# One of four weight sums of each gate/up set: from accumulating transfers to four GpSimd additions

## The chip, the core and the metric

The kernel runs on one core of a Trainium2 chip. The metric is the device time of one execution in microseconds (us), the median of several executions; lower is better. The engines are named as in the profile: PE is TensorE's matmul, PEld its weight loads, DVE is VectorE, ACT is ScalarE, POOL is GpSimd, SP is SyncE, which here only issues transfers.

## The reference

Two decoder layers over 256 tokens of width 1024 in float32. A layer adds to `h`, one after the other: half a SwiGLU feed-forward block (FFN1), a token mixer (differential attention in layer 0, a Mamba-2 scan in layer 1), a cross-attention into 256 memory tokens, and half a second SwiGLU block (FFN2). A last RMSNorm follows. There are thus four feed-forward blocks, and the change lies in them:

```
def rmsnorm(x, w):
    xf = x.astype(jnp.float32)
    y = xf * lax.rsqrt(jnp.mean(xf * xf, axis=-1, keepdims=True) + EPS)
    return (y * w.astype(jnp.float32)).astype(x.dtype)

def swiglu(h, w_gate, w_up, w_down):
    return (jax.nn.silu(h @ w_gate) * (h @ w_up)) @ w_down

    h = h + 0.5 * swiglu(rmsnorm(h, ffn1_norm[i]), ffn1_w_gate[i], ffn1_w_up[i], ffn1_w_down[i])
```

`w_gate` and `w_up` are 1024 x 2816, `w_down` is 2816 x 1024; all weights are read from DRAM once per execution, in float32.

## The kernel before

**Splitting.** A float32 product is made of three matmuls in a reduced format (L262 to L264): each operand is the sum of a `hi` and a `lo` part, and `hi*hi`, `hi*lo` and `lo*hi` are accumulated. A weight tile in SBUF, 128 x 2048 (`w`, L161, four blocks of 128 rows by 512 columns), is cut into *granules* of 128 x 1024. For each, ACT rounds the granule to `whi` (L224) and DVE subtracts it from the weights, `wlo = w - whi` (L225). PE then uses both. Four `whi` and four `wlo` buffers exist, so ACT and DVE can run some three granules ahead of PE, no more.

**Sets.** Gate and up projection are not multiplied one by one. For a group of 512 columns of each, `seven` makes a two by two block product with seven block products instead of eight: the columns of `w_up` are B11 (upper half of the rows) and B21 (lower half), those of `w_gate` are B12 and B22. Four sums of weights are needed:

- x1 = B11 + B12, by DVE into a new tile (L203, 128 x 2048, as soon as both are loaded);
- x2 = x1 + B22, by DVE in place (L203);
- x4 = x2 + B21, in x2's tile, by two transfers from DRAM that add to what lies in SBUF (L199, issued by POOL);
- x3 = B12 + B22, in B12's tile, by two such transfers as well (L199).

B22 is also loaded by itself (SP), since it is a factor of its own and the second operand of x2. The products come in the order B11, x1, x2, B22, x3, B21, x4, two granules each. Between these fourteen granules PE works on granules of other matrices ("hosts", `share` and `weave`): gate, up and down projection in ordinary form. There are 15 sets: three in the first FFN (column groups 2, 3, 4) and four in each other one (groups 1 to 4).

**What sets the order.** Each engine executes its own list in order. The lists come from the program order and a planner with due times (`pipe.after`), and are fixed when the kernel is built. Transfers into SBUF are issued by SP in its own order, each as soon as one of nine `w` buffers is free. POOL's list is short: the accumulating transfers, a power function on tiny tiles for the norms (L466, `rcol`), and additions in the attention (L930) and the scan (L1436 to L1440). DVE's list in a set holds, beside L203 and L225, operations that read a matmul result in PSUM: L831 and L837 (sums of products), L843 and L808 (gating), L859 (the `lo` part of the hidden activations).

Of the kernel before, what the change touches and what calls it, by code (L numbers as in the profile page):

```python
# [12 lines left out]
ALU = mybir.AluOpType  # L13
# [44 lines left out]
def trunk(ctx, tc, a, out):  # L58
    nc = tc.nc
# [15 lines left out]
    def acc(name):  # L75
        return pacc.tile([P, 512], F32, name=name, tag="acc")
# [4 lines left out]
    def work(name, n=512, dt=F32):  # L81

        return wk.tile([P, n], dt, name=name, tag="v", bufs=6) if n <= 256 else wk.tile([P, n], dt, name=name, tag="w")
# [24 lines left out]
    class Pipe:  # L108
# [4 lines left out]
        def after(self, us, f):  # L113
            self.q.append((self.t + us, f))
# [30 lines left out]
    class W:  # L145
# [6 lines left out]
        def load(self, k=None, nk=None):  # L152
            if k is None:
                if self.t is not None:
                    return
                k, nk = 0, self.nk
            if self.t is None:
                t = wp.tile([P, 2048], F32, name="w", tag="w")
                self.t = t[:, :self.nk * self.n].rearrange("p (k c) -> p k c", c=self.n)
            r0 = (self.k0 + k) * P  # L160
            nc.sync.dma_start(self.t[:, k:k + nk, :], self.src[r0:r0 + nk * P, self.c0:self.c0 + self.n]  # L161
                              .rearrange("(k p) c -> p k c", p=P))
# [17 lines left out]
    class Sum:  # L180
# [5 lines left out]
        def load(self):  # L186
            if self.t is not None:
                return
            self.l.load()
            if self.into is None:  # L190
                self.r.load()
                self.t = wp.tile([P, 2048], F32, name="w", tag="w").rearrange("p (k c) -> p k c", c=512)
            else:
                self.t = self.l.t
            w = self.r
            if self.into == "dma":
                for k in (0, 2):
                    r0 = (w.k0 + k) * P
                    nc.gpsimd.dma_start(self.t[:, k:k + 2, :], w.src[r0:r0 + 2 * P, w.c0:w.c0 + w.n]  # L199
                                        .rearrange("(k p) c -> p k c", p=P), accum_op=ALU.add)  # L200
            else:
                w.load()
                nc.vector.tensor_tensor(self.t, self.l.t, w.t, op=ALU.add)  # L203

    class Gran:

# [54 lines left out]
    def mm3(o, lh, ll, rh, rl, start, stop, onto=False):  # L261
        nc.tensor.matmul(o, lhsT=lh, rhs=rh, start=start, stop=False, skip_group_check=onto)  # L262
        nc.tensor.matmul(o, lhsT=lh, rhs=rl, start=False, stop=False, skip_group_check=onto)  # L263
        nc.tensor.matmul(o, lhsT=ll, rhs=rh, start=False, stop=stop, skip_group_check=onto)  # L264
# [93 lines left out]

    ONTO = {2: 0, 4: 0, 3: 1, 5: 1, 6: 1}

    def seven(b1, b2, x, mix, after, order=(0, 1, 2, 3, 5, 4, 6), second="dma"):

        b11, b21 = (W(b1[0], k, 4, b1[1], 512) for k in (0, 4))
        b12, b22 = (W(b2[0], k, 4, b2[1], 512) for k in (0, 4))
        x1 = Sum(b11, b12)
        x2 = Sum(x1, b22, second)
        x4 = Sum(x2, b21, "dma")
        x3 = Sum(b12, b22, "dma")
        banks = {}

        def a(t, h):
            return lambda k: tuple(v[:, t * P:(t + 1) * P] for v in pipe.need(x, 4 * h + k))

        def s(i):
            return lambda k: tuple(v[:, k * P:(k + 1) * P] for v in pipe.need(mix, i))
        plan = [(x1, s(0)), (b11, a(0, 0)), (b22, s(1)), (x2, s(2)), (b21, a(0, 1)), (x3, s(3)), (x4, a(1, 1))]
        out = []
        for i in order:
            w, lhs = plan[i]
            for k0 in (0, 2):  # L380
                def step(g, i=i, lhs=lhs, k0=k0):
                    if not k0:
                        banks[i] = banks[ONTO[i]] if i in ONTO else acc("seven")
                    for k in range(k0, k0 + 2):
                        lh, ll = lhs(k)
                        mm3(banks[i], lh, ll, g.hi[:, k - k0, :], g.lo[:, k - k0, :], k == 0 and i < 2, k == 3, onto=i in ONTO)
                        pipe.pe(0.68)
                    if k0:
                        for w in {0: (x2, x3), 3: (x4,)}.get(i, ()):
                            w.load()  # L390
                        after(i, banks)
                out.append((Gran(w.k0 + k0, 2, (w, 0, 512)), step))
        return out

    def share(hosts, s, counts):
        out, hosts = [], list(hosts)
        for i, n in enumerate(counts):
            out += hosts[:n] + s[2 * i:2 * i + 2]
            hosts = hosts[n:]
        return out + hosts  # L400
# [381 lines left out]
    def ffn_hidden(nm, l, norm, fin, tail, extra=None):  # L782
# [31 lines left out]
        def extras(c):  # L814
            for i in (2 * c, 2 * c + 1):
                if extra and i in extra:
                    extra[i]()

        def seven_fin(c):
            us, t = {}, {}  # L820

            def after(i, b):
                v = nc.vector

                def copy():
                    t[i] = work(f"p{i}")
                    nc.scalar.copy(t[i], b[i])

                def c12():
                    us[0] = t[3]  # L830
                    v.tensor_tensor(us[0], b[2], t[3], op=ALU.subtract)  # L831
                    nc.scalar.copy(b[2], t[1])
                    nc.scalar.activation(us[0], us[0], AF.Silu, scale=norm.col[:, 0:1])

                def c22():
                    us[1] = t[0]
                    v.tensor_tensor(t[0], t[0], b[5], op=ALU.subtract)  # L837
                    nc.scalar.activation(t[0], t[0], AF.Silu, scale=norm.col[:, 1:2])
                    if c == 4:
                        extras(6)  # L840

                def up(r):
                    v.scalar_tensor_tensor(us[r], b[i], norm.col[:, r:r + 1], us[r], op0=ALU.mult, op1=ALU.mult)  # L843
                    if r:
                        pipe.after(T["hid"], lambda: turn(c, [us[0], us[1]], 512))
                        extras(c)
                pipe.after(0.7, {0: copy, 1: copy, 3: copy, 2: c12, 5: c22, 4: lambda: up(0), 6: lambda: up(1)}[i])
            return after

        def turn(c, us, n):  # L850
            for i in range(0, n // P, 2):
                tp = v2(small_ps("htp"))
                for j in range(2):
                    for t in range(2):
                        nc.tensor.transpose(tp[:, j, t * P:(t + 1) * P], us[t][:, (i + j) * P:(i + j + 1) * P], ident)  # L855
                hi = v2(slot("hid_hi", F32R))
                lo = v2(slot("hid_lo", F32R))
                nc.scalar.copy(hi, tp)
                nc.vector.tensor_tensor(lo, tp, hi.bitcast(F32), op=ALU.subtract)  # L859
                for j in range(2):  # L860
                    hid[4 * c + i + j] = (hi[:, j, :], lo[:, j, :])
        wg, wu = a[nm + "_w_gate"][l], a[nm + "_w_up"][l]
        wide([(wg, 0, 512)], norm, "gate", gate_fin(0), **({} if units else dict(single=True, eng=nc.gpsimd)))
        c = HID // 512
# [19 lines left out]
            n += d0[i:j] + d1[i:j]  # L884
        steps = []
        for c, k in counts.items():
            s = seven((wu, c * 512), (wg, c * 512), norm.x, norm.s, seven_fin(c), (1, 0, 3, 2, 5, 4, 6), "dve")
            steps += share(n[:sum(k)], s, k)
            n = n[sum(k):]
        assert not n  # L890
# [3 lines left out]
    def ffn(nm, l, norm, nxt, extra=None):  # L894
        fin = upd(0.5, nxt)
        ffn_hidden(nm, l, norm, fin, lambda hid, wd: down(wd, 1, [(12, 4), (16, 4)], hid, [], 12, fin), extra)
# [218 lines left out]
    def cross_attention(l, norm, kv, nxt):  # L1115
# [86 lines left out]
        wkv = a["xa_w_kv"][l]  # L1202
        q = [g for c in (2, 0) for g in columns(a["xa_w_q"][l], c * 256, norm, "xq", [q_fin(c), q_fin(c + 1)])]
        weave(share(q, seven((wkv, 1024), (wkv, 1536), kv.x, kv.s, mv_fin()), [2, 1, 1, 2, 1, 1, 0]))
        out_b(a["xa_w_o"][l], KT, ot, upd(1.0, nxt), (4, 0))

# [329 lines left out]
    def last(norm):  # L1536
# [71 lines left out]
        def tail(hid_, wd):  # L1608
            hid.append(hid_)
            gr.extend(Gran(k, 2, (w, 0, 512)) for w in [W(wd, k, 4, 512, 512) for k in (12, 16)] for k in (w.k0, w.k0 + 2))  # L1610
            return [(gr[0], run)]
        ffn_hidden("ffn2", 1, norm, first_half, tail, {12: final_gain})
        units.append((gr[1:], run))

# [72 lines left out]
```

## Time and profile before

| | |
|---|---|
| median of 3 executions | 1257.75 us (1257.62 to 1258.05) |
| the profiled execution | 1258.38 us, of which the span is 1256.6 us |
| PE busy | 1247.1 us (99%), PEld 1071.7 us (85%) |
| DVE busy | 1057.2 us (84%) |
| ACT busy | 873.5 us (70%) |
| POOL busy | 162.5 us (13%) |
| transfers | 275.03 MB, of which 38.28 MB on the queue q0, which POOL feeds |
| granted TensorE clock | 0.999 |

A page of the profile gives busy time by engine, the span in 40 slices, the transfer queues, the chain of waits that ended last, groups of instructions by source line, and the transfers by issuer with their median time to landing. Other views show one engine's instructions in order of time, the waits added up by who waited for whom, and busy time within chosen windows. In a row of the timeline the first number is the start in us from the span's start, the second the duration, and what stands in brackets is the idle time of the engine before it and what ended that. Instructions that follow one another directly and have the same line and tiles are merged into one row, with their count.

### The profile page before, as it was taken

How to read it: one execution, taken by the hardware profiler on the slowest of the kernel's cores; microseconds unless marked ns; L12 is line 12 of the kernel's file. 1: busy time of each engine (PE TensorE's matmuls, PEld its weight loads, DVE VectorE, ACT ScalarE, POOL GpSimd, SP SyncE). 2: the span in 40 equal slices, each digit the busy share in tenths (PEclk: the TensorE clock that was granted, in tenths of full speed). 3: DMA queues.
4: the chain of work that ended last, by engine and by line, in shares of the span. 5: the costliest groups of instructions: out<-in, count | busy, mean ns of one | idle time of the engine just before them, and what ended most of it. 6: DMA issues, size and time to landing. Idle time of an engine off the chain costs nothing.

```text
span 1256.6 us, 18186 instructions
## 1 busy us (share of the span) xinstructions
PE 1247.1 (99%) x6751; PEld 1071.7 (85%) x6751; DVE 1057.2 (84%) x1451; ACT 873.5 (70%) x1388; POOL 162.5 (13%) x139
## 2 busy tenths in 40 slices
PE   9999999999999999999999999999999999999997
PEld 7888888788998888888888889999998898888886
DVE  6998787887787999887998976798898887898886
ACT  6676764686676776767776756777876775877772
POOL 1101102101101111110111000022233100011100
PEclk9999999999999999999999999999999999999999
DMA  9989976445776688987879977665636586489961
GB/s 330 301 255 259 314 256 208 137 165 170 222 214 170 165 252 260 293 246 234 240 198 268 311 247 221 192 193 168 201 134 185 169 246 182 157 251 256 258 190 34
DMA packets 161195, 275.03 MB, mean 219 GB/s; under 512 B 7209, under 2 KB 43730, under 8 KB 161106
## 3 DMA queue, kind: packets, MB, share of 16 engines
q1 hardware_dynamic: 137744, 229.75, 53.4%
q0 software_dynamic: 19744, 38.28, 17.7%
q10 hardware_dynamic: 3618, 5.84, 1.4%
q8 instruction: 53, 0.87, 0.3%
q14 instruction: 36, 0.29, 0.1%
HBM read 271.72 MB, written 2.13 MB: 218 GB/s over the span
## 4 chain that ended last, share of the span: by engine, by line
PE 94%; DMA 2%; DVE 2%; ACT 2%; issue 1%; POOLq 0%; POOL 0%; SPq 0%; ACTq 0%; DVEq 0%
PE out L262 9%; PE out L264 9%; PE out L263 9%; PE seven L263 8%; PE seven L262 8%; PE seven L264 8%; PE htp L855 1%; PE up L263 1%; PE up L264 1%; PE up L262 1%; PE xs L264 1%; PE xs L262 1%; PE xq L263 1%; PE xq L264 1%; PE xs L263 1%; PE xq L262 1%
## 5 line engine op out<-in xcount | busy, mean ns | idle before, releaser
L225 DVE TENSOR_TENSOR wlo<-w,whi 128x1024 fp32r<-128x1024 f32 (+2 forms) x532 | 639.4, 1220 | 134.6 <-ACT whi L224 126.8
L224 ACT CAST whi<-w 128x1024 fp32r<-128x1024 f32 (+2 forms) x534 | 551.0, 1039 | 245.2 <-PE out L264 84.0
L262 PE MATMUL out<-whi,hid_hi 128*128 128x512 f32 x336 | 132.3, 394 | 0.0
L264 PE MATMUL out<-whi,hid_lo 128*128 128x512 f32 x336 | 131.0, 390 | 0.0
L263 PE MATMUL out<-wlo,hid_hi 128*128 128x512 f32 x336 | 130.8, 389 | 0.0
L263 PE MATMUL seven<-wlo,s_hi 128*128 128x512 f32 x272 | 106.0, 390 | 0.6 <-DVE wlo L225 0.6
L262 PE MATMUL seven<-whi,s_hi 128*128 128x512 f32 x272 | 106.2, 390 | 0.0
L264 PE MATMUL seven<-whi,s_lo 128*128 128x512 f32 x272 | 105.9, 389 | 0.0
L199 POOL DMA_DIRECT2D w<-in_ffn_w_up_dram x30 | 36.7, 1268 | 346.6 <-DVE wlo L225 339.5
L203 DVE TENSOR_TENSOR w<-w 128x2048 f32<-128x2048 f32 x32 | 73.2, 2287 | 2.0 <-DMA w<-in_ffn_w_gate_dram 1.5
L264 PEld LDWEIGHTS out<-whi,hid_lo 128*128 128x128 f32 x336 | 63.1, 188 | 13.4
L263 PEld LDWEIGHTS out<-wlo,hid_hi 128*128 128x128 f32 x336 | 63.1, 188 | 12.6
L262 PEld LDWEIGHTS out<-whi,hid_hi 128*128 128x128 f32 x336 | 63.1, 188 | 12.5
L262 PE MATMUL seven<-whi,xh 128*128 128x512 f32 x180 | 70.5, 392 | 0.0
L264 PE MATMUL seven<-whi,xl 128*128 128x512 f32 x180 | 70.1, 389 | 0.0
L263 PE MATMUL seven<-wlo,xh 128*128 128x512 f32 x180 | 70.0, 389 | 0.0
L263 PEld LDWEIGHTS seven<-wlo,s_hi 128*128 128x128 f32 x272 | 51.1, 188 | 11.4 <-DVE wlo L225 1.0
L264 PEld LDWEIGHTS seven<-whi,s_lo 128*128 128x128 f32 x272 | 51.1, 188 | 10.7
L262 PEld LDWEIGHTS seven<-whi,s_hi 128*128 128x128 f32 x272 | 51.1, 188 | 10.4
L199 POOL DMA_DIRECT2D w<-in_ffn_w_gate_dram x30 | 36.9, 1467 | 176.2 <-DVE xst L1146 62.3
L264 PEld LDWEIGHTS seven<-whi,xl 128*128 128x128 f32 x180 | 33.8, 188 | 7.1
L262 PEld LDWEIGHTS seven<-whi,xh 128*128 128x128 f32 x180 | 33.8, 188 | 6.8
(395 smaller groups left out, 3013.7 us busy)
## 6 DMA issues: line engine op xcount, KB each, us to landing
w<-in_ffn_w_up_dram SPq DMA_DIRECT2D x40, 1024.0 KB, 7.8
w<-in_ffn_w_down_dram SPq DMA_DIRECT2D x40, 1024.0 KB, 9.3
w<-in_ffn_w_gate_dram SPq DMA_DIRECT2D x38, 1024.0 KB, 8.9
w<-in_ssd_w_in_dram SPq DMA_DIRECT2D x24, 1024.0 KB, 5.4
w<-in_xa_w_kv_dram SPq DMA_DIRECT2D x16, 1024.0 KB, 6.4
w<-in_ffn_w_gate_dram POOLq DMA_DIRECT2D x30, 512.0 KB, 9.7
w<-in_ffn_w_up_dram POOLq DMA_DIRECT2D x30, 512.0 KB, 7.2
w<-in_da_w_in_dram SPq DMA_DIRECT2D x12, 1024.0 KB, 5.2
```

Of the source, the lines that this page charges most:

```text
L199: nc.gpsimd.dma_start(self.t[:, k:k + 2, :], w.src[r0:r0 + 2 * P, w.c0:w.c0 + w.n] .rearrange("(k p) c -> p k c", p=P), accum_op=ALU.add)
L203: nc.vector.tensor_tensor(self.t, self.l.t, w.t, op=ALU.add)
L224: nc.scalar.copy(hv, src)
L225: self.eng.tensor_tensor(self.lo[:, :, o:o + n], src, hv.bitcast(F32), op=ALU.subtract)
L262: nc.tensor.matmul(o, lhsT=lh, rhs=rh, start=start, stop=False, skip_group_check=onto)
L263: nc.tensor.matmul(o, lhsT=lh, rhs=rl, start=False, stop=False, skip_group_check=onto)
L264: nc.tensor.matmul(o, lhsT=ll, rhs=rh, start=False, stop=stop, skip_group_check=onto)
L855: nc.tensor.transpose(tp[:, j, t * P:(t + 1) * P], us[t][:, (i + j) * P:(i + j + 1) * P], ident)
```

## The change

x3 is no longer made by two accumulating transfers of 512 KB each. POOL adds the loaded B22 to B12's tile itself, in four steps of 128 x 512.

```diff
@@ class Sum, load
             else:
                 w.load()
-                nc.vector.tensor_tensor(self.t, self.l.t, w.t, op=ALU.add)
+                if self.into != "pool":
+                    nc.vector.tensor_tensor(self.t, self.l.t, w.t, op=ALU.add)
+                    return
+                for k in range(4):
+                    nc.gpsimd.tensor_tensor(self.t[:, k, :], self.t[:, k, :], w.t[:, k, :], op=ALU.add)
@@
-    def seven(b1, b2, x, mix, after, order=(0, 1, 2, 3, 5, 4, 6), second="dma"):
+    def seven(b1, b2, x, mix, after, order=(0, 1, 2, 3, 5, 4, 6), second="dma", third="dma"):
...
-        x3 = Sum(b12, b22, "dma")
+        x3 = Sum(b12, b22, third)
...
-            s = seven((wu, c * 512), (wg, c * 512), norm.x, norm.s, seven_fin(c), (1, 0, 3, 2, 5, 4, 6), "dve")
+            s = seven((wu, c * 512), (wg, c * 512), norm.x, norm.s, seven_fin(c), (1, 0, 3, 2, 5, 4, 6), "dve",
+                      "pool")
```

POOL's list in layer 0's FFN2, in the first three sets of that block, before the change: w_4298, w_4589 and w_4898 are tiles of B12 that become x3, the others those of x1, x2 and x4.

```order
L199 DMA w_4298<-in_ffn2_w_gate_dram 128x2x512 x2
L466 TENSOR_TENSOR rcol_4186<-msq_4184,neghalf_94 128x2
L199 DMA w_4300<-in_ffn2_w_up_dram 128x2x512 x2
L199 DMA w_4589<-in_ffn2_w_gate_dram 128x2x512 x2
L199 DMA w_4591<-in_ffn2_w_up_dram 128x2x512 x2
L199 DMA w_4898<-in_ffn2_w_gate_dram 128x2x512 x2
```

The same place with the change (w_4304, w_4597 and w_4908 are the tiles of B12, and the last operand of an L207 row is the loaded B22):

```order
L207 TENSOR_TENSOR w_4304<-w_4304,w_4360 128x512 x4
L470 TENSOR_TENSOR rcol_4192<-msq_4190,neghalf_94 128x2
L199 DMA w_4306<-in_ffn2_w_up_dram 128x2x512 x2
L207 TENSOR_TENSOR w_4597<-w_4597,w_4658 128x512 x4
L199 DMA w_4599<-in_ffn2_w_up_dram 128x2x512 x2
L207 TENSOR_TENSOR w_4908<-w_4908,w_4971 128x512 x4
```

In all 15 sets the two transfers give way to four additions at the same place of POOL's list, 60 additions for 30 transfers; nothing else on POOL moves.

DVE's list around x2's sum, in the second set of layer 0's FFN2, with the change (L204 is the sum, L203 before; L229 is L225 before; w_4658 is B22):

```order
L229 TENSOR_TENSOR wlo_4542<-w_4306,whi_4541 128x1024
L847 SCALAR_TENSOR_TENSOR p3_4425<-seven_4351,rcol_4192,p3_4425 128x512
L229 TENSOR_TENSOR wlo_4559<-w_4560,whi_4558 128x1024
L229 TENSOR_TENSOR wlo_4571<-w_4560,whi_4570 128x1024
L229 TENSOR_TENSOR wlo_4581<-w_4582,whi_4580 128x1024
L847 SCALAR_TENSOR_TENSOR p0_4385<-seven_4291,rcol_4192,p0_4385 128x512
L229 TENSOR_TENSOR wlo_4596<-w_4599,whi_4595 128x1024
L229 TENSOR_TENSOR wlo_4610<-w_4599,whi_4609 128x1024
L204 TENSOR_TENSOR w_4599<-w_4599,w_4658 128x2048
L863 TENSOR_TENSOR hid_lo_4630<-htp_4624,hid_hi_4629 128x512
L863 TENSOR_TENSOR hid_lo_4639<-htp_4633,hid_hi_4638 128x512
L229 TENSOR_TENSOR wlo_4646<-w_4582,whi_4645 128x1024
```

It is the list of before with other tile numbers: on PE, DVE, ACT and SP the change leaves every instruction in its place. What an instruction waits for differs: an addition to B12's tile waits for the landing of B22, which the transfer did not; ACT's reading of x3 waits for POOL instead of the transfers; x4's transfers stand behind the additions on POOL.

## The prediction, made before the changed kernel ran

> **What bounds the kernel now.** I read the page first, then the waits of PE, then windows around nine of the sets.
>
> ```profile
> span 1256.6 us, 18186 instructions
> PE 1247.1 (99%) x6751; PEld 1071.7 (85%) x6751; DVE 1057.2 (84%) x1451; ACT 873.5 (70%) x1388; POOL 162.5 (13%) x139
> ```
>
> ```profile
> PE warm L597 <- DVE warm L99: 1.5, 1, 1.5
> PE seven L263 <- DVE wlo L225: 0.6, 1, 0.6
> PE acs L1285 <- PE mk L264: 0.2, 1, 0.2
> ```
>
> The three rows are the whole list of PE's waits (total, times, longest): 2.3 us in 1256.6. The kernel is bound by PE's own instructions, so the change cannot make it faster by more than about those 2.3 us; the part that lies in a set is 0.6. What it can do is make PE wait. The windows below (432 to 466 is the second set of layer 0's FFN2; the last row adds up nine such stretches; columns: length, then busy time and count of PE, PEld, DVE, ACT, POOL) say who is next:
>
> ```profile
> 432.00:466.00 34.00, 34.00 (x159) 28.31 (x158) 32.34 (x34) 25.78 (x31) 4.91 (x4) 1.00 0.88 260
> sum 337.00, PE 337.00 PEld 279.91 DVE 307.88 ACT 243.86 POOL 57.61; mean PE 37.44 PEld 31.10 DVE 34.21 ACT 27.10 POOL 6.40
> ```
>
> PE has no gap; DVE is busy 32.34 of 34 us, and over the nine stretches idle (337.00 - 307.88) / 9 = 3.2 us per set. DVE, which makes every `wlo`, is the engine that must not lose time in a set.
>
> **What it removes.** Thirty accumulating transfers, 30 x 512 KB = 15.7 MB of this queue's 38.28:
>
> ```profile
> q0 software_dynamic: 19744, 38.28, 17.7%
> w<-in_ffn_w_gate_dram POOLq DMA_DIRECT2D x30, 512.0 KB, 9.7
> ```
>
> That is 15.7 / 38.28 x 17.7% = 7% of the transfer engines' time, an estimate. It frees transfer time that PE does not wait for: no row of its waits names a DMA. Gain: 0, at most the 0.6 us.
>
> **What it adds.** Sixty additions of 128 x 512 on POOL, which is 87% idle. The nearest row has the same form (float32, two inputs and the output in SBUF, in place), the attention's L930. What such an addition costs DVE shows where the two meet (POOL's and DVE's timelines, rows in order of time):
>
> ```profile
> L930 POOL TENSOR_TENSOR rt<-rt,rt x8: 1277/1304/2272, 202.4 to 246.1; 128x512 f32<-128x512 f32 x8
> 245.54 0.41 DVE L929 TENSOR_TENSOR rt<-k,cossinr 128x256 f32<-128x256 f32 x1
> 244.87 1.30 POOL L930 TENSOR_TENSOR rt<-rt,rt 128x512 f32<-128x512 f32 x1 [12.35 <-DVE rt L929]
> 245.87 1.38 DVE L225 TENSOR_TENSOR wlo<-w,whi 128x1024 fp32r<-128x1024 f32 x1
> 246.12 2.27 POOL L930 TENSOR_TENSOR rt<-rt,rt 128x512 f32<-128x512 f32 x1
> 247.18 2.30 DVE L225 TENSOR_TENSOR wlo<-w,whi 128x1024 fp32r<-128x1024 f32 x1
> 821.04 1.04 POOL L1440 TENSOR_TENSOR xn<-xn,dskh 128x512 f32<-128x512 f32 x1
> ```
>
> They take turns. POOL's first addition ends at 246.17; the `wlo` that began at 245.87 ends at 247.25, 1.08 us after that, where it usually takes 1.22 in all. POOL's second addition began at 246.12 and ends at 248.39, 1.14 after that `wlo`; the next `wlo`, begun at 247.18, ends at 249.48, 1.09 after the addition. So an addition and a subtraction whose two inputs lie in SBUF exclude one another: one runs, the other stands. The addition holds DVE for 1.15 us; a `wlo` starts needing the shared way 0.13 after its start (1.22 - 1.09). An operation with a PSUM input is not held: L929, from PSUM, took 0.41 in the middle of the addition, as without one. Bounds of the hold: the whole 1.30 of the free addition from above; from below 0.89, since L1440, with one operand that repeats, took 1.04 in all, less the same 0.15 of start.
>
> The Trainium skill says so too (SBUF — State Buffer, Who interferes with whom): a DVE instruction with two SBUF inputs and a GpSimd instruction that reads SBUF exclude each other for the whole instruction, whichever starts first. By that rule taken literally, 1.30 per addition, the sum below comes to 1281; by the rows, which show 1.15, to 1274. The rows decide.
>
> **One set, step by step** (432 to 466). The additions can begin when B22 has landed: it was issued at 434.8 and took 10.0, so 444.8. POOL is free by then.
>
> ```profile
> L161 SPq DMA_DIRECT2D w<-in_ffn_w_gate_dram x1: 368/368/368, 434.8 to 434.8; - x1
> DMA to landing us min/median/max: 10.0/10.0/10.0
> ```
>
> ```profile
> 444.93 0.68 DVE L837 TENSOR_TENSOR p<-p,seven 128x512 f32<-128x512 f32 x1
> 445.52 2.35 DVE L225 TENSOR_TENSOR wlo<-w,whi 128x1024 fp32r<-128x1024 f32 x2
> 447.79 0.74 DVE L843 SCALAR_TENSOR_TENSOR p<-seven,rcol,p 128x512 f32<-128x512 f32 x1
> 448.45 1.21 DVE L225 TENSOR_TENSOR wlo<-w,whi 128x1024 fp32r<-128x1024 f32 x1
> 450.58 2.54 DVE L225 TENSOR_TENSOR wlo<-w,whi 128x1024 fp32r<-128x1024 f32 x2 [0.91 <-ACT whi L224]
> 453.04 0.74 DVE L843 SCALAR_TENSOR_TENSOR p<-seven,rcol,p 128x512 f32<-128x512 f32 x1
> 453.70 2.35 DVE L225 TENSOR_TENSOR wlo<-w,whi 128x1024 fp32r<-128x1024 f32 x2
> 456.08 2.29 DVE L203 TENSOR_TENSOR w<-w 128x2048 f32<-128x2048 f32 x1
> 458.29 1.28 DVE L859 TENSOR_TENSOR hid_lo<-htp,hid_hi 128x512 fp32r<-128x512 f32 x2
> 459.49 1.21 DVE L225 TENSOR_TENSOR wlo<-w,whi 128x1024 fp32r<-128x1024 f32 x1
> 461.28 0.39 PE L263 MATMUL gateup<-wlo,xh 128*128 128x512 f32 x1
> ```
>
> - Addition 1, 444.80 to 445.95, lies mostly beside L837 (PSUM input). The first `wlo` would need the way from 445.65: 0.30 late, ends 447.04.
> - Addition 2, 447.04 to 448.19. The second `wlo` would go on at 447.09: 1.10 more, 1.40 late, ends 449.27.
> - Addition 3, 449.27 to 450.42, beside L843. The third `wlo` loses 0.44: 1.84 late. Then 0.91 idle takes up as much: 0.93.
> - Addition 4, 451.50 to 452.65. The fourth `wlo` loses 1.01: 1.94 late. So of 4 x 1.15 = 4.60, what lies beside PSUM work, idle time and starts is 2.66.
>
> Behind that DVE has no idle time up to 459.49: two granules, x2's own sum of 2.29, two L859. The `wlo` of 459.49 ends at 460.70, and PE's first matmul with it starts at 461.28: a lead of 0.58, the low point of a set, since x2's sum has used up the lead. PE will wait 1.94 - 0.58 = 1.36 us. In terms of the hold h it is 4h - 3.24: 0.32 at 0.89, 1.96 at 1.30, nothing below 0.81.
>
> **All sets.** The low point is the same elsewhere; in the last set the `wlo` begins at 1200.65, ends at 1201.87, and is needed at 1202.40, a lead of 0.53:
>
> ```profile
> 1200.65 1.22 DVE L225 TENSOR_TENSOR wlo<-w,whi 128x1024 fp32r<-128x1024 f32 x1
> 1202.40 0.39 PE L263 MATMUL out<-wlo,hid_hi 128*128 128x512 f32 x1
> ```
>
> Not so in the first set of the three later FFNs. In layer 0's FFN2 B22 was issued at 387.1 and landed 6.8 later, 29 us before x2's sum, where DVE idles before every second granule. There the delay is taken up at once: 0.
>
> ```profile
> L161 SPq DMA_DIRECT2D w<-in_ffn_w_gate_dram x1: 368/368/368, 387.1 to 387.1; - x1
> DMA to landing us min/median/max: 6.8/6.8/6.8
> 393.42 1.22 DVE L225 TENSOR_TENSOR wlo<-w,whi 128x1024 fp32r<-128x1024 f32 x1 [1.24 <-ACT whi L224]
> 396.14 1.23 DVE L225 TENSOR_TENSOR wlo<-w,whi 128x1024 fp32r<-128x1024 f32 x1 [1.50 <-ACT whi L224]
> 406.93 0.71 POOL L466 TENSOR_TENSOR rcol<-msq,neghalf 128x2 f32<-128x2 f32 x1 [21.58 <-DVE msq L464]
> ```
>
> That leaves 12 sets. I take the one walked through for all: 12 x 1.36 = 16.3 us. The profiled execution took 1258.38: 1274.7; it was 0.6 over the median, so **1274** against 1257.75. With the bounds of the hold: 12 x 0.32 = 4 gives 1262, 12 x 1.96 = 23.5 gives 1281.
>
> **Waits that are new, and cost nothing.** Behind the additions on POOL stand x4's transfers and, in the three first sets, the norm's `rcol`. The walked set's additions end at 452.65; x4's transfers went out at 462.21: 9.6 us of cover. `rcol` began at 406.93, when its input came; additions from 393.9 on, at most 2.3 apart (1.15 and a `wlo`), end by 403.1. Tightest is the first FFN's first set, where x1's sum ends only at 48.51 and x4's transfers begin at 58.42: 48.51 + 4 x 2.3 = 57.7.
>
> ```profile
> 462.21 2.45 POOL L199 DMA_DIRECT2D w<-in_ffn_w_up_dram  x2 [26.92 <-DVE wlo L225]
> 46.22 2.29 DVE L203 TENSOR_TENSOR w<-w 128x2048 f32<-128x2048 f32 x1
> 58.42 2.42 POOL L199 DMA_DIRECT2D w<-in_ffn_w_up_dram  x2 [6.99 <-issue]
> ```
>
> Without that cover each set would pay what the transfers are late, at most the 9 us of four alternating additions. With fewer transfers in flight B22 may land in 6.8 rather than 10.0 us; the additions then begin at 441.6, among the same kind of rows, and the loss stays.
>
> **Rivals.**
> 1. *No change.* The exclusion is real, but idle time takes up the delay before the low point, as in the first sets: DVE idles 3.2 us per set against 1.94 of delay. It decides where the hold is under 0.81 us or B22 lands so early that all four additions meet idle gaps. Against it: the idle time lies mostly elsewhere, 0.91 of it in the walk. Time 1257 to 1260.
> 2. *Much slower.* If the additions fall where nothing lies beside them, right ahead of x2's sum, a set loses 4.60 - 0.58 = 4.0, 12 sets 48 us: about 1306; half of that 1282. For it: nothing in the walked stretch from 453 to 459 is idle. Against: B22 landed 11 us before the sum, and will not land later with less traffic.
> 3. *Faster.* The freed 7% of transfer time ends PE waits that have a transfer as their cause. It decides if PE waited for landings; its list of waits has none, so 1255.5 at best.
>
> **How the numbers follow.** The forecast, slower by 4 to 24 us (1262 to 1282), gets 0.75, rival 2 0.08, rival 1 0.14, rival 3 0.03. A measurement tells 0.2%, 2.5 us, from no change. Rivals 1 and 3 mostly stay within that: faster 0.02, same 0.15, slower 0.83. The range runs from 1259, into rival 1, to 1283.
>
> **What would show it.** In the changed profile L225's longest durations should rise above 2 us in the sets; POOL's additions should take 1.3 to 2.3 us each, not 1.3 throughout; PE should wait for `wlo` right after x2's sum, in some 12 places of 1 to 2 us, and for nothing else; B22 should land sooner. If L225's mean stays at 1.22, the exclusion does not hold here and the forecast is wrong. If PE waits elsewhere, for x3 or x4, the queue on POOL was the cause and not DVE.

## The result and the profile after

The changed kernel takes **1278.5 us** (1277.64 to 1280.04, median of 4 runs) against 1257.85 us (1257.62 to 1258.05) for the kernel before: a ratio of 1.0165, with a 95% interval of 1.0150 to 1.0181. It is slower, as forecast, by 20.7 us where 16.3 were forecast. The time lies inside the range (1259 to 1283). The profiled execution took 1277.64 us, 19.3 us more than that of the kernel before (1258.38).

From the page of the changed kernel: the span, the busy times, the transfers that POOL feeds, the two groups of instructions that the argument is about, and the loads of gate weights (KB each, and us to landing). The lines of the code have moved: `whi` is L228, `wlo` L229, DVE's sums L204, POOL's additions L207.

```profile
span 1275.8 us, 18168 instructions
PE 1255.2 (98%) x6751; PEld 1068.4 (84%) x6751; DVE 1094.3 (86%) x1451; ACT 872.8 (68%) x1388; POOL 246.2 (19%) x169
q0 software_dynamic: 11584, 22.55, 10.5%
L229 DVE TENSOR_TENSOR wlo<-w,whi 128x1024 fp32r<-128x1024 f32 (+2 forms) x532 | 676.6, 1294 | 116.4 <-ACT whi L228 110.1
L207 POOL TENSOR_TENSOR w<-w 128x512 f32<-128x512 f32 x60 | 120.5, 2037 | 288.8 <-DVE wlo L229 111.7
w<-in_ffn_w_gate_dram SPq DMA_DIRECT2D x38, 1024.0 KB, 6.2
```

Two of these rows as they were in the kernel before:

```profile
L225 DVE TENSOR_TENSOR wlo<-w,whi 128x1024 fp32r<-128x1024 f32 (+2 forms) x532 | 639.4, 1220 | 134.6 <-ACT whi L224 126.8
w<-in_ffn_w_gate_dram SPq DMA_DIRECT2D x38, 1024.0 KB, 8.9
```

The same 1451 DVE instructions are busy 37.1 us longer (1094.3 against 1057.2), and that is `wlo`: its group is busy 37.2 us longer (676.6 against 639.4), with a mean of 1294 ns in place of 1220. POOL's additions take 2.04 us in the mean. The queue q0 carries 15.7 MB less, as said, and the loads of gate weights land 6.2 us after their issue in place of 8.9. That relief bought PE nothing directly, since PE had waited for no transfer; what PE waits for now stands in the view of its waits (total us, times, longest):

```profile
PE out L267 <- DVE wlo L229: 4.4, 6, 2.0
PE seven L267 <- DVE wlo L229: 2.3, 5, 0.8
PE seven L266 <- ACT whi L228: 1.6, 1, 1.6
PE warm L601 <- DVE warm L99: 1.5, 1, 1.5
PE gate L331 <- ACT whi L228: 1.2, 1, 1.2
PE gateup L267 <- DVE wlo L229: 0.7, 2, 0.5
PE gate L267 <- DVE wlo L229: 0.6, 1, 0.6
PE xt L539 <- DVE h L587: 0.5, 2, 0.3
```

Where there was one wait of 0.6 us for `wlo` there are now 14, together 8.0 us, two for DVE's `h`, and one of 1.6 us for ACT's `whi`. (The other one for `whi`, 1.2 us, lies at 7 us, long before the first addition, and is not the change's.) None names a transfer, x3 or x4. Not all of the loss shows in this list: PE's busy time is 8.1 us longer as well (1255.2 against 1247.1), since a PE whose `wlo` comes late by a little runs its matmuls further apart without a wait that the view records.

So the loss was also read from PE's instructions one by one. Both kernels give PE the same 6751 in the same order; the start of the n-th in the one, less that of the n-th in the other, is the delay there, and its growth over a stretch is what that stretch lost:

| sets | forecast, us | measured, us |
|---|---|---|
| three of the first FFN | 3 x 1.36 = 4.1 | 3.3 + 2.8 + 2.7 = 8.8 |
| first set of the three later FFNs | 0 | 0.5 + 0.2 + 0.4 = 1.1 |
| the other nine | 9 x 1.36 = 12.2 | 9.7 (from 0.1 to 2.0 each) |
| between the sets | 0 | -0.3 |
| all | 16.3 | 19.3 |

### The profile page after: what moved, and what is told of

Same layout as the page of the kernel before. It is cut to its first block, busy times and chain, and to the rows that moved or that the text cites. A ratio compares the mean times of both kernels' runs of the same rounds, so it can differ in the third digit from the quotient of the medians.

```text
span 1275.8 us, 18168 instructions
## 1 busy us (share of the span) xinstructions
PE 1255.2 (98%) x6751; PEld 1068.4 (84%) x6751; DVE 1094.3 (86%) x1451; ACT 872.8 (68%) x1388; POOL 246.2 (19%) x169
## 4 chain that ended last, share of the span: by engine, by line
PE 82%; DVE 11%; issue 4%; ACT 2%; DMA 1%; POOLq 0%; POOL 0%; DVEq 0%; ACTq 0%; SPq 0%
PE out L267 8%; PE out L268 8%; PE out L266 8%; DVE wlo L229 7%; PE seven L267 6%; PE seven L268 6%; PE seven L266 6%; DVE w L204 2%; PE xs L268 2%; PE xs L266 2%; PE xs L267 2%; PE mk L266 1%; PE xq L267 1%; PE xq L268 1%; PE mk L268 1%
## 5 line engine op out<-in xcount | busy, mean ns | idle before, releaser
L229 DVE TENSOR_TENSOR wlo<-w,whi 128x1024 fp32r<-128x1024 f32 (+2 forms) x532 | 676.6, 1294 | 116.4 <-ACT whi L228 110.1
L228 ACT CAST whi<-w 128x1024 fp32r<-128x1024 f32 (+2 forms) x534 | 550.4, 1039 | 261.4 <-PE out L268 75.5
L207 POOL TENSOR_TENSOR w<-w 128x512 f32<-128x512 f32 x60 | 120.5, 2037 | 288.8 <-DVE wlo L229 111.7
L204 DVE TENSOR_TENSOR w<-w 128x2048 f32<-128x2048 f32 x32 | 74.2, 2320 | 3.3 <-DMA w<-in_ffn_w_gate_dram 2.6
L267 PEld LDWEIGHTS seven<-wlo,xh 128*128 128x128 f32 x180 | 33.8, 188 | 12.0 <-DVE wlo L229 5.5
```

The costliest lines, as they stand in the source:

```text
L207: nc.gpsimd.tensor_tensor(self.t[:, k, :], self.t[:, k, :], w.t[:, k, :], op=ALU.add)
L228: nc.scalar.copy(hv, src)
L229: self.eng.tensor_tensor(self.lo[:, :, o:o + n], src, hv.bitcast(F32), op=ALU.subtract)
```

## The experiments

The expectations call the runs by short names: extra_adds, write_only, one_add, not_first and late_adds are the first five below, in this order. Theory 1 in them is the prediction's: an addition on POOL and a DVE instruction with two inputs in SBUF exclude one another. Its rivals are that the loss comes from POOL's queue (x4's transfers stand behind the additions) or from transfers. 1a and 1b are two readings within theory 1: by 1a it matters where in a set the additions lie; by 1b the transfers themselves cost time once DVE is short.

### The additions beside the old transfers

The kernel before, with 60 additions of 128 x 512 that read the landed B22 and write a scratch tile; x3 still comes by its transfers. This is the price of the additions without what the removed transfers give back.

```diff
+    junk_t = const.tile([P, 512], BF16, name="padd")
...
+                if self.extra:
+                    w.load()
+                    for k in range(4):
+                        nc.gpsimd.tensor_tensor(junk_t, w.t[:, k, :], w.t[:, 3 - k, :], op=ALU.add)
```

> The kernel before, x3 still made by the accumulating transfers, and in each set four more additions of 128 x 512 on GpSimd at the place where the change has them; they read the loaded B22 twice and write to a scratch tile that nobody reads. Theory 1 (an addition that reads SBUF shuts out DVE's operations with two SBUF inputs): the loss is all or nearly all there, 1258 + 17 to 22, so 1275 to 1280, and L225's mean rises from 1.22 to about 1.29 us as with the change. Theory 2 (x3, x4 or a buffer comes late because it now depends on GpSimd): x3 does not depend on the additions here, 1258 to 1262, at most x4's transfers stand behind them. Theory 3 (the missing transfers move the loads and so the whole schedule): no transfer is missing, 1258.

Measured: 1290.87 us (1290.21 to 1292.20), ratio 1.0262 (1.0245 to 1.0279). The scratch additions alone cost 33 us, more than the change as a whole. The groups and the waits of this kernel:

```profile
L231 DVE TENSOR_TENSOR wlo<-w,whi 128x1024 fp32r<-128x1024 f32 (+2 forms) x532 | 682.1, 1303 | 123.5 <-ACT whi L230 118.5
L206 POOL TENSOR_TENSOR padd<-w 128x512 bf16<-128x512 f32 x60 | 121.7, 2029 | 141.3 <-DMA w<-in_ffn_w_gate_dram 137.8
PE out L269 <- DVE wlo L231: 12.9, 9, 2.0
```

The additions and `wlo` are stretched as in the changed kernel (2029 and 1303 ns), so a loss of this kind arises without any part of x3. But the forecast for this run was too low by over 10 us, and the difference to the changed kernel says that the removed transfers gave something back that the prediction had at nothing.

### The same time on POOL, without reading

Ten fills of the scratch tile in each set in place of the four additions, after a tiny addition that waits for B22. POOL is busy for 250.8 us in all, in the changed kernel for 246.2, with x4's transfers behind the fills; but the fills read nothing.

```diff
+                if self.extra:
+                    w.load()
+                    nc.gpsimd.tensor_tensor(junk_t[:, 0:2], w.t[:, 0, 0:2], w.t[:, 3, 0:2], op=ALU.add)
+                    for k in range(10):
+                        nc.gpsimd.memset(junk_t, 0.0)
```

> As extra_adds, but with ten fills of the scratch tile by GpSimd in each set in place of the four additions, behind one addition of 2 elements per partition that waits for B22. The fills write SBUF and read nothing. Theory 1, if it is the reading that shuts DVE out: 1258 to 1260, L225's mean stays 1.22. If any GpSimd work on SBUF does it: a loss in proportion to GpSimd's busy time, over 5 us. Theory 2: x4's transfers stand behind the fills as they did behind the additions, so the same loss as in extra_adds.

Measured: 1257.67 us, ratio 1.0000 (0.9991 to 1.0010). The groups of this kernel:

```profile
L232 DVE TENSOR_TENSOR wlo<-w,whi 128x1024 fp32r<-128x1024 f32 (+2 forms) x532 | 639.0, 1219 | 134.5 <-ACT whi L231 126.5
L207 POOL MEMSET padd<- 128x512 bf16 x150 | 79.3, 528 | 8.6
```

79.3 us of fills, in the same places, leave `wlo` at 1219 ns and the time where it was. POOL's time and its queue cost nothing here; what costs is that its instruction reads SBUF.

### One long addition

The changed kernel with one addition of 128 x 2048 per set in place of four of 128 x 512.

```diff
-                for k in range(4):
-                    nc.gpsimd.tensor_tensor(self.t[:, k, :], self.t[:, k, :], w.t[:, k, :], op=ALU.add)
+                nc.gpsimd.tensor_tensor(self.t, self.t, w.t, op=ALU.add)
```

> The change with one addition of 128 x 2048 in each set in place of four of 128 x 512. Theory 1 with the exclusion for the whole instruction: DVE stands once for some 4.5 us in each set, PSUM work beside it hides about 0.7; the lead of 0.6 to 3 us that PE has then is gone at once, 2.5 to 3.2 us per set in 12 sets, and something in the three others: 1290 to 1300, and single wlo or sums of 5 to 6 us in DVE's rows. If the two engines shared the way element by element or piece by piece: as the change, 1276 to 1281, and no wlo over 3.5 us. Theory 2: as the change.

Measured: 1296.17 us (1294.80 to 1301.18), ratio 1.0313 (1.0291 to 1.0335). The additions' group and the largest group of PE's waits in its profiled execution, the slowest of the four:

```profile
L206 POOL TENSOR_TENSOR w<-w 128x2048 f32<-128x2048 f32 x15 | 73.0, 4870 | 288.2 <-DMA w<-in_ffn_w_gate_dram 141.0
PE seven L266 <- DVE wlo L228: 18.6, 10, 3.7
```

Once begun, an addition holds the way to its end: a `wlo` caught behind it loses up to 4.4 us, where the same elements in four pieces let a `wlo` through between two. The holder keeps it per instruction, not per element.

### Later FFNs only

The changed kernel, with the first FFN's three sets as before.

```diff
-                      "pool")
+                      "dma" if norm is first_norm else "pool")
```

> The change in the 12 sets of the three later FFNs; the first FFN's three sets keep the accumulating transfers. Set against the kernel before along PE's own instructions, the changed kernel lost 8.8 us in the first FFN's three sets and 10.2 in the other twelve. If the losses are local (theory 1): 1258 + 10 = 1268. If the first FFN's delay, or its lighter traffic, makes the later ones: outside 1266 to 1270.

Measured: 1268.84 us (1268.37 to 1269.21), ratio 1.0088 (1.0073 to 1.0104). The twelve later sets lose about what they lose in the changed kernel (by PE's starts 11.4 us together, there 10.8), and the first FFN nothing. The loss is local: what the later FFNs cost does not depend on the first. Three of fifteen sets thus make up nearly half of the loss.

### The additions 4 us later

The changed kernel, with a pause of five fills ahead of the additions (tied by two tiny additions, so that they can't be passed).

```diff
+                nc.gpsimd.tensor_tensor(junk_t[:, 0:2], w.t[:, 0, 0:2], w.t[:, 0, 0:2], op=ALU.add)
+                for k in range(5):
+                    nc.gpsimd.memset(junk_t, 0.0)
+                nc.gpsimd.tensor_tensor(self.t[:, :, 0], self.t[:, :, 0], junk_t[:, 0:4], op=ALU.add)
                 for k in range(4):
```

> The change with a pause of about 4 us on GpSimd (five fills of a scratch tile, which cost nothing above, and two tiny additions) between B22's landing and the four additions of each set. Question: why did the additions cost 33 us in extra_adds and 21 in the change. There they began 9 to 13 us before x2's sum in most sets of the later FFNs, here 13 to 17, since B22 lands sooner where the x3 transfers are missing. Theory 1a, the distance decides, because idle time of DVE between the additions and the sum takes up the delay: with 4 us less distance the loss comes near that of extra_adds, 1284 to 1293. Theory 1b, the transfers themselves cost time once DVE is short (x3 or the loads come late): the change's time, 1277 to 1281.

Measured: 1283.58 us (1283.07 to 1284.48), ratio 1.0205 (1.0190 to 1.0220): 5 us more than the changed kernel, between the two expectations. In a later FFN's other sets the additions began 9.0 to 14.3 us ahead of x2's sum, in the changed kernel 13 to 17. So it does matter where they lie, and this is what the removed transfers gave back: B22 lands sooner, and the delay has longer to be taken up. It accounts for some 5 of the 12 us between the changed kernel and the one with scratch additions. There the additions began 9.2 to 13.8 us ahead of x2's sum, nearly as here, and cost 7 us more. These lie mostly in the first FFN (13.5 us lost there with scratch additions, 9.3 here) and in the fourth set of the second FFN (4.1 and 2.5). One piece can be seen in the first set of all (7.6 and 5.2), in DVE's and POOL's rows of the kernel with scratch additions:

```profile
50.08 4.14 DVE L231 TENSOR_TENSOR wlo<-w,whi 128x1024 fp32r<-128x1024 f32 x1 [0.58 <-ACT whi L230]
49.22 2.61 POOL L201 DMA_DIRECT2D w<-in_ffn_w_gate_dram  x2 [27.95 <-DVE w L209]
```

The addition behind these transfer issues was recorded from 50.88 to 53.13. A `wlo` that had begun 0.8 us ahead of it stood until it had ended, and lost 2.9 us, where one addition otherwise costs 1.1. An issue alone does not do that: the 76 `wlo` beside POOL's transfer issues in the kernel before took at most 1.23 us. Why it happened here, and the rest of the 7 us, stays open.

### The additions apart

As in "Later FFNs only", with four fills (about 3.5 us with their two ties) between one addition and the next.

```diff
                 for k in range(4):
                     nc.gpsimd.tensor_tensor(self.t[:, k, :], self.t[:, k, :], w.t[:, k, :], op=ALU.add)
+                    if k < 3:
+                        pause(self.t[:, k, 0:2], self.t[:, k + 1, 0:2], 4)
```

> As not_first (additions in the 12 sets of the later FFNs, 1268.8 us), with a pause of some 3.5 us of fills and two tiny additions on GpSimd between one addition and the next. Theory 1a: each addition makes DVE up to 1.15 late, and the idle time in between takes up a part of it, so less arrives at x2's sum: 1259 to 1265. If only the number of additions that meet DVE's work counts, not their distance: 1267 to 1271. The fourth addition comes some 16 us after B22's landing, about when x2's sum begins; where it falls behind the sum, at the low point, it costs up to 0.6 us.

Measured: 1265.85 us (1263.76 to 1266.50), ratio 1.0060 (1.0045 to 1.0075), 3 us less than without the pauses and just above what 1a expected. The gain is small because the stretched run of additions meets other things. In six sets the last addition met x2's sum and took 3.2 to 3.4 us. And the first set of the third FFN lost 2.3 us where it had lost 0.3; there POOL was the one that stood, with a tie of two elements per partition:

```profile
587.80 6.25 POOL L186 TENSOR_TENSOR w<-w,padd 128x2 f32<-128x2 f32 x1
```

It ended with a run of twelve DVE instructions that followed one another without a gap. The norm's `rcol`, behind it on POOL, came late (595.4 us, 586.4 without the pauses), ACT stood 3.9 us for it, and PE waited in the end. So POOL's queue can cost, though it does not in the changed kernel.

### Half by POOL, half by transfer

Two additions in each set; the other half of x3 comes by one accumulating transfer.

```diff
-                for k in range(4):
+                r0 = (w.k0 + 2) * P
+                nc.gpsimd.dma_start(self.t[:, 2:4, :], w.src[r0:r0 + 2 * P, w.c0:w.c0 + w.n]
+                                    .rearrange("(k p) c -> p k c", p=P), accum_op=ALU.add)
+                for k in range(2):
```

> The change with half of it: in each set two of the four blocks of x3 are added by GpSimd, the other two by one accumulating transfer. By the step by step sum of the prediction two additions make DVE 0.30 + 1.10 = 1.40 late, 0.91 idle takes up most of it, and 0.49 is under the lead of 0.58: nothing arrives in the 12 sets of the later FFNs; in the first FFN's three sets, which have no such slack, about half of their 8.8: 1258 to 1264, and L225's mean half way, 1.25 to 1.26. If the loss is in proportion to the additions: 1258 + 10 = 1268.

Measured: 1268.63 us (1266.51 to 1269.23), ratio 1.0082 (1.0067 to 1.0097), in the bracket of proportional loss and not in the lower one. By place the answer differs. In its profiled execution (span 1264.7 us) the twelve later sets lost 1.5 us together, almost nothing, as the prediction's walk says of two additions: the delay after the second is 1.40 us, the idle 0.91 leaves 0.49 of it, and the lead of 0.58 covers that. (That execution, 1266.51 us, is the fastest of the four and 2.1 below their median.) The first FFN lost 7.0 us of the 8.8 that four additions cost: 2.9, 0.6 and 3.6 in its three sets. PE's waits for it, and DVE's and POOL's rows in the third set:

```profile
PE seven L270 <- DVE wlo L232: 5.4, 3, 2.7
120.26 4.40 DVE L232 TENSOR_TENSOR wlo<-w,whi 128x1024 fp32r<-128x1024 f32 x1
119.83 1.20 POOL L207 DMA_DIRECT2D w<-in_ffn_w_gate_dram  x1 [16.19 <-DVE w L204]
120.58 2.98 POOL L210 TENSOR_TENSOR w<-w 128x512 f32<-128x512 f32 x2
```

This one `wlo` stood through both additions, although it had begun 0.3 us ahead of the first, and lost 3.2 us; one in the first set stood through both as well and lost 2.9. That is nearly all that the two sets lost. It is the case of the scratch additions again, an addition right behind a transfer issue on POOL, so most of the 7.0 us is not what two additions cost by themselves.

### DVE makes the sum itself

x3 by DVE, 15 more sums of 128 x 2048, none by POOL. (The lists of DVE, ACT and PE differ from the changed kernel's in a few places.)

```diff
-                      "pool")
+                      "dve")
```

> x3 made by DVE itself, as x2 is: one sum of 128 x 2048 per set, no transfer and no GpSimd addition; the planner puts most of these sums close behind x2's. It shows what the same work costs as DVE's own. The changed kernel's DVE was busy 37 us longer than before; 15 sums of 2.28 are 34. Theory 1: DVE's time is what counts, so a loss of the same order, 1265 to 1284, more where the sum sits right behind x2's (2.28 - 0.58 = 1.7 per set, 25 us). If GpSimd as such is the trouble (its queue, its dependences): 1258 to 1262.

Measured: 1269.92 us (1268.93 to 1272.66), ratio 1.0093 (1.0076 to 1.0110). The sums' group in this kernel:

```profile
L204 DVE TENSOR_TENSOR w<-w 128x2048 f32<-128x2048 f32 x47 | 107.4, 2286 | 11.6 <-DMA w<-in_ffn_w_gate_dram 11.4
```

15 sums of 2.29 us are 34 us of DVE's own time, and cost 12. Four additions of 1.15 us hold are up to 4.6 us of DVE's time per set against 2.29 for doing the work. As measured, DVE's busy time grew by 28.1 us here (1085.3 against 1057.2), with the sums, and by 37.1 in the changed kernel, without them. With additions of this size the work was not taken off DVE: it was charged to DVE at 1.3 times its price, and cost 21.

### The additions cut smaller

The changed kernel with eight additions of 128 x 256 per set, and with sixteen of 128 x 128. Each reads the same elements in all.

```diff
-                for k in range(4):
-                    nc.gpsimd.tensor_tensor(self.t[:, k, :], self.t[:, k, :], w.t[:, k, :], op=ALU.add)
+                for k in range(8):
+                    c = slice(k % 2 * 256, k % 2 * 256 + 256)
+                    nc.gpsimd.tensor_tensor(self.t[:, k // 2, c], self.t[:, k // 2, c], w.t[:, k // 2, c], op=ALU.add)
```

> The changed kernel with each set's sum cut into eight additions of 128x256 in place of four of 128x512; the same elements are read. Theory A, the hold goes by the elements read: each addition holds VectorE's two-operand instructions about 0.55 us in place of 1.15, the loss per set stays near 8 x 0.55 = 4.4 us of VectorE less what it catches up, so the time stays within 4 us of the changed kernel's 1278.5 us: 1275 to 1282. Theory B, a fixed part in each addition counts as well (its start, or the exchange of the port with VectorE, about 0.1 us each): 8 x 0.65 = 5.2 us per set, 1282 to 1290. Theory C, shorter holds slip between VectorE's instructions and only part of them is charged: 1266 to 1274.

> The changed kernel with each set's sum cut into sixteen additions of 128x128; the same elements are read. Eight additions of 128x256 came to 1270.9 us against 1278.5 with four. Theory A, the shorter a hold the more of it falls into VectorE's idle time, its PSUM operations and its starts: 1263 to 1268. Theory B, halving gains nothing more, because each addition brings a fixed part (16 holds of about 0.3 us are as much as 8 of 0.57): 1268 to 1274. Theory C, alternating with VectorE's instructions, each addition waits about 1 us for its turn, so sixteen take about 20 us, reach into x2's sum and put off x4's transfers: over 1274, with PE waits that name a DMA or ACT's copies of x4.

Measured: eight, 1270.94 us (1269.45 to 1272.89), ratio 1.0107 (1.0090 to 1.0124); sixteen, **1261.70 us** (1261.26 to 1262.34), ratio 1.0027 (1.0015 to 1.0038). From the page and the waits of the kernel with sixteen:

```profile
PE 1249.2 (99%) x6751; PEld 1070.6 (85%) x6751; DVE 1073.0 (85%) x1451; ACT 873.0 (69%) x1388; POOL 353.4 (28%) x349
L230 DVE TENSOR_TENSOR wlo<-w,whi 128x1024 fp32r<-128x1024 f32 (+2 forms) x532 | 654.8, 1250 | 121.0 <-ACT whi L229 115.7
L208 POOL TENSOR_TENSOR w<-w 128x128 f32<-128x128 f32 x240 | 228.1, 986 | 283.3 <-DMA w<-in_ffn_w_gate_dram 128.2
PE seven L268 <- DVE wlo L230: 1.0, 1, 1.0
```

The size of a piece is the strongest lever found, and the first expectation for sixteen (1263 to 1268) was not low enough. The table puts the four sizes beside each other; the loss of `wlo` is summed over those 128 x 1024 `wlo` of a trace that overlap an addition, each less 1.22 us.

| additions per set | shortest one, us | `wlo` that met one | their loss, us | DVE busy, more than before, us | time, more than before, us |
|---|---|---|---|---|---|
| 1 of 128 x 2048 | 4.58 | 23 | 58.7 | 54.7 | 38 |
| 4 of 128 x 512 | 1.29 | 63 | 40.0 | 37.1 | 21 |
| 8 of 128 x 256 | 0.72 | 88 | 33.2 | 29.6 | 13 |
| 16 of 128 x 128 | 0.45 | 125 | 16.9 | 15.8 | 3 |

In these four kernels they take turns: the longest loss of a `wlo` is one hold (4.4 us with one addition, 1.10 with four, 0.58 with eight, 0.32 with sixteen), while an addition waits for a whole `wlo`. (The two cases right behind a transfer issue and POOL's 6.25 us, above, show that it need not be so everywhere.) Cut smaller, the sum loses time on POOL, which has it to spare, and DVE loses at most one short hold at a time. The same set as the prediction's, with sixteen (DVE's and POOL's timelines):

```profile
441.69 15.67 POOL L208 TENSOR_TENSOR w<-w 128x128 f32<-128x128 f32 x16 [9.35 <-DMA w<-in_ffn_w_gate_dram]
447.46 2.71 DVE L230 TENSOR_TENSOR wlo<-w,whi 128x1024 fp32r<-128x1024 f32 x2
450.75 1.23 DVE L230 TENSOR_TENSOR wlo<-w,whi 128x1024 fp32r<-128x1024 f32 x1
452.35 2.86 DVE L230 TENSOR_TENSOR wlo<-w,whi 128x1024 fp32r<-128x1024 f32 x2 [0.36 <-ACT whi L229]
458.48 2.29 DVE L204 TENSOR_TENSOR w<-w 128x2048 f32<-128x2048 f32 x1
```

POOL needs 15.67 us for the sum where four additions need 8.01, and ends just ahead of x2's sum. Pairs of `wlo` take 2.71 and 2.86 in place of 2.35 us, one takes its usual 1.23, and the set loses 0.3 us. In other sets the sixteen run into x2's sum, which then takes up to 2.55 us. This is still slower than the kernel before; with 2.3 us of waits on a PE that is 99% busy there was nothing to win.

## Why the prediction was right, and where its terms were off

**What bounds, and the sign: right.** PE had no slack to give, DVE was next, and PE's new waits are for `wlo`.

**The exclusion and its hold of 1.15: shown.** The changed kernel's instructions of the two lines (shortest, median and longest in ns):

```profile
L207 POOL TENSOR_TENSOR w<-w x60: 1286/2268/2360, 48.3 to 1208.0; 128x512 f32<-128x512 f32 x60
L229 DVE TENSOR_TENSOR wlo<-w,whi x532: 213/1218/2318, 7.2 to 1258.9; 128x1024 fp32r<-128x1024 f32 x174, 128x512 fp32r<-128x512 f32 x2, 128x768 fp32r<-128x768 f32 x1, 128x64 fp32r<-128x64 f32 x1
```

An addition takes 1.29 us alone and 2.27 in the median, and the longest `wlo` 2.32, as in the attention's rows. The fills show that reading is what excludes; the single long addition, that the hold lasts as long as the instruction. The Trainium skill (SBUF — State Buffer, Who interferes with whom) gives the same rule, exclusion for the whole instruction, and the run with 4.87 us per addition agrees. "Whichever starts first", as the prediction has it, did not hold for two `wlo` behind a transfer issue: they began 0.3 us (two additions per set) and 0.8 us (scratch additions) ahead of the addition and still stood. The rule's literal hold of 1.30 would have brought the sum to 1281 and the rows' 1.15 to 1274; the time fell between, but not by the hold: the per-set losses differ from each other far more than the two holds do.

**The walked set: 0.8 us where 1.36 were forecast.** The changed kernel's rows there (POOL, then DVE):

```profile
448.97 8.01 POOL L207 TENSOR_TENSOR w<-w 128x512 f32<-128x512 f32 x4 [9.47 <-DVE p L835]
450.08 5.74 DVE L229 TENSOR_TENSOR wlo<-w,whi 128x1024 fp32r<-128x1024 f32 x3
456.35 2.85 DVE L229 TENSOR_TENSOR wlo<-w,whi 128x1024 fp32r<-128x1024 f32 x2
459.78 3.48 DVE L229 TENSOR_TENSOR wlo<-w,whi 128x1024 fp32r<-128x1024 f32 x3
466.22 2.29 DVE L204 TENSOR_TENSOR w<-w 128x2048 f32<-128x2048 f32 x1
```

The additions begin 17.3 us ahead of x2's sum; the walk had them begin 11.3 ahead of it in the old frame (456.08 - 444.80). The transfer of B22 took about 5 us and not 10.0 (loads issued by SP in this stretch):

```profile
DMA to landing us min/median/max: 5.0/5.1/5.1
```

Five `wlo` in the first two DVE rows above lose 5.74 + 2.85 less 5 usual ones (3.48 + 2.35), 2.76 us together; three more, at their usual 3.48, run without the idle 0.91 that the kernel before had here. The prediction considered the early landing and said that the loss stays. That was wrong by 0.5 us in this set and 2.5 over the nine. The late additions show the direction: put later, so that they begin 14.3 us ahead of x2's sum, they cost this set 1.6 us.

**The low point behind x2's sum: half right.** The prediction had PE wait right behind x2's sum, in some 12 places of 1 to 2 us, and for nothing else. Of the 14 waits for `wlo`, seven begin some 5 us after the start of an x2 sum, 0.2 to 2.0 us each. The other seven, 0.2 to 0.6 us each, lie ahead of it or at its start, while additions run or within 1.2 us of their end. By PE's starts, 4.9 of the nine sets' 9.7 us were lost before x2's sum began. PE's lead is short in more places than the one that was walked to.

**The first FFN: the term that failed.** "I take the one walked through for all" gave its three sets 4.1 us; they lost 8.8. In the walked set B22 landed 12 us after the end of x1's sum (432.46); in these three sets of the changed kernel the additions begin 0.1 to 0.5 us behind it. The first set of the kernel before, on DVE:

```profile
49.68 3.60 DVE L225 TENSOR_TENSOR wlo<-w,whi 128x1024 fp32r<-128x1024 f32 x3 [0.58 <-ACT whi L224]
53.20 2.28 DVE L203 TENSOR_TENSOR w<-w 128x2048 f32<-128x2048 f32 x1
56.66 5.77 DVE L225 TENSOR_TENSOR wlo<-w,whi 128x1024 fp32r<-128x1024 f32 x5 [1.17 <-ACT whi L224]
```

And in the changed kernel, on POOL, DVE and PE:

```profile
48.31 8.00 POOL L207 TENSOR_TENSOR w<-w 128x512 f32<-128x512 f32 x4 [27.23 <-DVE w L204]
49.40 5.75 DVE L229 TENSOR_TENSOR wlo<-w,whi 128x1024 fp32r<-128x1024 f32 x3 [0.57 <-ACT whi L228]
55.08 3.38 DVE L204 TENSOR_TENSOR w<-w 128x2048 f32<-128x2048 f32 x1
59.62 6.95 DVE L229 TENSOR_TENSOR wlo<-w,whi 128x1024 fp32r<-128x1024 f32 x6 [1.17 <-ACT whi L228]
59.64 0.50 PE L266 MATMUL seven<-whi,s_hi 128*128 128x512 f32 x1 [1.64 <-ACT whi L228]
```

The additions begin as soon as x1's sum is made, and x2's sum follows after only three granules. The three `wlo` lose 2.15 us, and the sum itself, which also has two inputs in SBUF, 1.10. The idle 1.17 us behind it stays as long as it was. It looks like slack, but it is ACT's `whi` of x2, which waits for the very sum that is late, so it moves along. Idle time takes up a delay only where what ends it is not itself behind the delay. For this set that is close to rival 2's case (additions right ahead of x2's sum, up to 4.0 us per set).

In the two other sets x2's sum itself is not held. The second lost most of its 2.8 us behind that sum, as in the walk, but with 0.18 us of idle time on the way where the walked set had 0.91. The third lost all of its 2.7 us ahead of x2's sum, right behind x1's. One `wlo` there with its use, in the kernel before (DVE, PE), and the same use in the changed kernel (PE):

```profile
117.86 1.22 DVE L225 TENSOR_TENSOR wlo<-w,whi 128x1024 fp32r<-128x1024 f32 x1
119.72 0.39 PE L263 MATMUL out<-wlo,hid_hi 128*128 128x512 f32 x1
127.26 0.50 PE L267 MATMUL out<-wlo,hid_hi 128*128 128x512 f32 x1 [0.57 <-DVE wlo L229]
```

This `wlo` ended 0.64 us ahead of its use, a lead as short as the 0.58 behind x2's sum. x1's sum, also 2.29 us of DVE's time, has a low point behind it as well, and the prediction counted only the other.

**The first sets of the later FFNs: 1.1 us in place of 0.** Idle time takes up most of the delay there, not all: in two of them PE waited for DVE's `h`.

**Nothing from the freed transfers: wrong in how it works.** They end no wait of PE, as said, but B22's earlier landing moves the additions, and the run with the transfers kept costs 12 us more. About 5 of these are shown to be the position; of the rest, a `wlo` that stood through a transfer issue and an addition is one piece, and the remainder is open.

**x4's transfers and `rcol` behind the additions: right, no cost.** No wait names them in the changed kernel, and the fills, in the same place on POOL, cost nothing. With the additions apart, `rcol` did come late.

The errors partly cancelled: 4.7 us too little for the first FFN, 1.1 for the first sets, 2.5 too much for the nine others. What bounds, the exclusion and its size were right; that the total came as near as it did is in part luck.

## What to carry to other kernels

In this kernel, work given to GpSimd beside a busy VectorE was free where it did not read SBUF. Where it does, price it as VectorE's time, from a place in the trace where the two already meet, and compare it with VectorE doing the work itself. Where it must be there, cut it into short instructions and start it early: the same sum cost 38 us as one piece per set, 21 as four and 3 as sixteen. Before idle time is counted as cover for a delay, look at what ends it: a wait for something that is itself delayed covers nothing. And look for every place where the lead is short, not only the shortest.

## What was not expected of the hardware

- The side that is cut small loses little: sixteen additions of 0.45 us per set, 240 in all, cost the 125 `wlo` that met them 16.9 us, some 46 of them about 0.3 us and some 45 none, although the 128 x 512 additions cost theirs 40.0. Why so many lose nothing was not tried.
- Taking turns has exceptions: a `wlo` stood through two additions right behind a transfer issue on POOL (3.2 us lost), and a tiny GpSimd addition stood 6.25 us beside a dozen VectorE instructions.
- VectorE doing the sum itself (34 us more work) cost 12 us; GpSimd doing it in four pieces per set cost 21.
- Fewer accumulating transfers, 15.7 MB of 275, go with other loads that land much sooner: gate weights in 6.2 in place of 8.9 us. A part may be the slower pace: with the scratch additions and all transfers kept they took 7.4.
